# Which engine makes the low parts of split weights: GpSimd and VectorE together, or VectorE alone

## The chip, the cores and the metric

The kernel runs on one core of a Trainium2 chip. The metric is device time in microseconds (us), the median of three runs; the profile comes from one further execution, whose own time is given beside it. Five engines work at once, each with its own queue of instructions, which it takes in order: TensorE (PE in the rows; PEld is its loading of weights), VectorE (DVE), ScalarE (ACT), GpSimd (POOL) and SyncE (SP), which here only starts transfers from memory.

## The reference, cut to what matters

256 rows of width 1024 go through two blocks of two layers each, all in float32.

```python
def first_block(x, mem, ...):
    for l in range(2):
        h = rms_norm(x, mix_norm_g[l])
        u, v, q, k, vv = split(h @ w_in[l])
        gm = gmlp_group(gelu(u), gelu(v), ...)
        at = gqa_group(q, k, vv, q_norm_g, k_norm_g, cos, sin)   # normed, rotated, softmax
        x = x + concat(rms_norm(gm), rms_norm(at)) @ w_out[l]
        x = x + memory_cross_attention(rms_norm(x), mem_n, ...)
        x = x + expert_choice_moe(rms_norm(x), ...)              # 16 experts
def second_block(x, c, ...):
    for l in range(2):
        sh1, sc1, g1, ... = split(silu(c) @ w_mod[l] + b_mod[l])
        x = x + 0.5 * g1 * swiglu(rmsnorm(x) * (1 + sc1) + sh1, ffn1 weights)
        x = x + g2 * hybrid_mixer(rmsnorm(x) * (1 + sc2) + sh2, ...)
        x = x + 0.5 * g3 * swiglu(rmsnorm(x) * (1 + sc3) + sh3, ffn2 weights)
```

The hybrid mixer multiplies the normed rows by w_in and feeds three groups of heads: stick-breaking attention, dilated attention (q and k normed by head and rotated, then three softmax patterns in one) and a gated recurrence (HGRN2), whose decays are worked out in seven levels of halving distance.

## The kernel before, in words

**Split products.** A dense product of two float32 matrices is made of three matrix products in a faster format: `mm3` (L134 to L140) adds high by high (L138), the one operand's low part by the other's high part (L139), and high by low (L140). A weight comes from memory in pieces of 1 MB (128 partitions of 2048 numbers) into a slot of a ring (`load`, L82). `split_w` (L108 to L132) cuts a piece into four parts of 128x512: ScalarE copies each into the high part (`wh`, L126), and VectorE or GpSimd subtracts that from the slot to give the low part (`wl`, L129). The high and low tiles come from a pool of 7 pairs in the first block and 8 in the second: a new pair waits until TensorE has done the products of the pair 7 or 8 places before it. The experts' weights are used unsplit, so they have no low parts.

**Who makes the low parts.** `lo_engines` (L94 to L103) gives the four engines of a piece. A pattern in `lo_on["first"]` is used once; else `lo_on["pool"]` pieces go to GpSimd whole; else the next letter of `lo_on["w"]` counts, V for VectorE, P for GpSimd, M for taking turns. `norm_T`, the norm ahead of a dense product, sets `lo_on["pool"]` to 1 (NP), so the first piece behind it goes to GpSimd.

**What else is on these engines.** VectorE also runs the chains of small operations ahead of attention: `root` (an inverse square root by three rounds of L185 to L189 on tiles of 128x1, 128x16 or 128x20), the diagonal matrices of a norm (L312, `diag`, which TensorE multiplies by the rows at L322), the put-away of a norm's result (L263, L265), the rotation (L567 to L589 in the first block, L1155 to L1169 in the hybrid mixer), the softmax's scaling (L501, L1207, `xn`) and the recurrence's products (L1289, L1290) and masked copies into the score matrix (L1273, L1300, `ST`). GpSimd also makes the recurrence's differences (L1286, L1287), the last sums of the row of modulations (L431), small powers (L176) and starts small transfers.

**Order.** A scheduler puts each engine's instructions into an order when the kernel is built, by its own estimates of durations; the code only names some that must come behind others (`queued`). An engine never passes a waiting instruction.

Of the kernel before, what the change touches and what calls it, by code (L numbers as in the profile page):

```python
# [34 lines left out]
L1, L2, NP = 1, 2, 1  # L35
# [6 lines left out]
def kernel(ctx: ExitStack, tc: tile.TileContext, A: dict, out: bass.AP, phases=None):  # L42
    nc = tc.nc
    V, ACT, PE, POOL = nc.vector, nc.scalar, nc.tensor, nc.gpsimd
# [9 lines left out]
    def dense_scope(stack, name):  # L54

        scope["split"] = stack.enter_context(tc.tile_pool(name=f"split{name}", bufs=8, reuse_waits="tile"))
        h = stack.enter_context(tc.tile_pool(name=f"h{name}", bufs=1, reuse_waits="tile"))
        scope["h"], scope["turn"] = [h, h], 0
# [29 lines left out]
    lo_on = {"w": "VP", "n": 0, "t": 0}  # L88
# [179 lines left out]
    def hl(name):  # L268
        pools, i = scope["h"], scope["turn"]
        scope["turn"] = 1 - i  # L270
        return tuple(
            pools[i].tile([P, KC, S], F32R, tag="hT" + e, name=uid(name + e), bufs=1 + (pools[0] is pools[1]))
            for e in "hl"
        )
# [24 lines left out]
    def norm_T(src, g, sh=None, gap=0, site="b", by_row=True, pre=None, row=None):  # L299


        h = hl("hT")
        lo_on["pool"] = NP
        dg = []
        sqs = h[1].rearrange("p (t n k) s -> p t n (k s)", t=2, n=2)
        if row is None:
# [210 lines left out]
    def mix(l, kT, v):  # L517
        with tc.tile_pool(name=f"mix{l}", bufs=1, reuse_waits="tile") as wk:
            w = A["w_in"][l]
            lo_on["first"] = 'PPVV'  # L520
            h, pre = raw_T(
                x, vec[:, 8 * l : 8 * l + 8], GM * l, l == 0, lambda: weights(w, 0, KC, 1536, 256)
            )
# [33 lines left out]
            if l == 0:  # L557
                mh, _ = norm_T(mem_load(), vec[:, 32:40], site="e")
# [468 lines left out]
    def late_init(pool):  # L1027

        t = pool.tile([P, NLATE], F32, name="late")
        POOL.dma_start(out=t, in_=A["const"][:, NKEEP:])  # L1030
        masks = pool.tile([P, NMASK], U8, name="masks").rearrange("p (n t) -> p n t", n=8)
        m = slot()[:, :NMASK]
        POOL.dma_start(out=m, in_=A["masks"])
        V.tensor_copy(masks, m.rearrange("p (n t) -> p n t", n=8))
        take = taker(t)
        return [take(P), take(P), masks] + [take(n, t=2) for n in (2 * S, 2 * S, 64, 64)]
# [24 lines left out]
    def ffn(l, name, q):  # L1061
        ms, mc = mod[l]
        wg, wu, wd = (A[f"{name}_w_{e}_2"][l] for e in ("gate", "up", "down"))
        with tc.tile_pool(name=f"{name}{l}", bufs=2, reuse_waits="tile") as wk:
            scale, row, gap = mc[:, 8 * q + 8 : 8 * q + 16], None, GB
            if l == q == 0:
                scale = small.tile([P, KC], F32, tag="gsc", name="gsc", bufs=1)
                V.tensor_tensor(scale, vec[:, 88:96], mc[:, 8:16], ALU.mult)
                row, gap = final_row[0], GF
            h, pre = norm_T(x, scale, mc[:, 8 * q : 8 * q + 8], gap, "b", q != 6, lambda: columns(wg, 0), row)  # L1070
            g = wk.tile([P, D], F32, tag="gate", name=uid("gate"), bufs=1)
            acc = [ps("acc") for _ in range(4)]
# [45 lines left out]
    def hybrid(l, tables):  # L1118
        ms, mc = mod[l]
        tri, sbneg, masks, dil_c, dil_neg, d_cos, d_sin = tables  # L1120
        w = A["w_in_2"][l]
        with tc.tile_pool(name=f"hyb{l}", bufs=1, reuse_waits="tile") as wk:
            h, pre = norm_T(
                x, mc[:, 32:40], mc[:, 24:32], max(GB, due(32 + 36 * l)), "h",
                pre=lambda: weights(w, 0, 4, 768, 512),
# [309 lines left out]
    side = {KV0: kv_begin} | {KV0 + 1 + i: kv_step(i) for i in range(8)}  # L1435

    for l in range(2):
        lo_on["w"] = 'VPVPVPVPVPVPVPVPVPVPVPVPVPV'
        lo_on["n"] = 0
        with ExitStack() as more:  # L1440
            with ExitStack() as st:
                split = st.enter_context(tc.tile_pool(name=f"split{l}", bufs=7, reuse_waits="tile"))
# [33 lines left out]
    with ExitStack() as st:  # L1476
        late = st.enter_context(tc.tile_pool(name="late", bufs=1, reuse_waits="tile"))
        dense_scope(st, "b")
        for l in range(2):
            lo_on["w"] = "V"  # L1480
            ffn(l, "ffn1", 0)
            if l == 0:
                tables = late_init(late)
            lo_on["w"] = 'VVVPVPVPVVVVVVVMVV'
            lo_on["n"] = 0
            hybrid(l, tables)
            lo_on["w"] = "V"
            ffn(l, "ffn2", 6)
# [119 lines left out]
```

## Time and profile before

| | |
|---|---|
| three runs, median (lowest to highest) | 2527.57 us (2526.87 to 2528.56) |
| the profiled execution: its own time, its span | 2528.26 us, 2526.2 us |
| busy: TensorE, VectorE, ScalarE, GpSimd | 86%, 49%, 39%, 19% |
| mean granted clock of TensorE | 0.918 |

By place, in us from the span's start: the first layer's mixer and cross attention take 0 to 240, its experts 240 to 735; the second layer's mixer and cross attention 735 to 912, its experts to 1385. In the second block the parts ffn1, hybrid mixer, ffn2 end at 1575, 1755 and 1950 in the first layer, and at 2153, 2332 and 2526 in the second. A row of the timeline gives start, duration, engine, line, operation, tiles and count, and in brackets how long the engine had been idle and what ended that. A row of waits gives engine, line, what was waited for, the sum in us, how many times, and the longest. Matmul ends are modelled, so a chain of matmuls is read from their starts.

### The profile page before, as it was taken

The numbers are of one execution on the slowest core, as the hardware profiler recorded it, in microseconds if no ns is written. First come the engines' busy times: TensorE is split into PE (matmuls) and PEld (weight loads), VectorE is DVE, ScalarE is ACT, GpSimd is POOL, SyncE is SP. The second block draws the span as 40 slices with busy tenths as digits, with TensorE's granted clock in tenths as the row PEclk, the third lists the DMA queues.
The fourth block names the chain that finished last, engine by engine and source line by source line (L and its number), as shares of the span: only waits on it lengthen the run. The fifth ranks groups of instructions, "written<-read, shape, count | busy, mean of one in ns | idle before, by whom it ended". The sixth has DMA issues, their size and how long they took to land.

```text
span 2526.2 us, 39105 instructions
## 1 busy us (share of the span) xinstructions
PE 2164.4 (86%) x15752; PEld 1614.4 (64%) x15752; DVE 1236.4 (49%) x2295; ACT 975.2 (39%) x1830; POOL 484.4 (19%) x328
## 2 busy tenths in 40 slices
PE   7898867787686987766667999999999999889999
PEld 6787424443165853212213998877998999777998
DVE  6755101000055531000003986877895986877655
ACT  5553110000044521000003774555764864545654
POOL 5141000000031300000001641231641550241100
PEclk9999979888888999878778999899999999989999
DMA  7367999999971789999997885424885785523652
GB/s 282 104 264 317 396 419 420 420 419 420 420 310 65 287 353 419 420 420 420 420 420 311 318 299 197 167 78 153 305 298 180 297 293 193 187 95 137 232 185 84
DMA packets 100214, 721.37 MB, mean 286 GB/s; under 512 B 11471, under 2 KB 11599, under 8 KB 12993
## 3 DMA queue, kind: packets, MB, share of 16 engines
q1 hardware_dynamic: 98640, 715.70, 72.5%
q0 software_dynamic: 1104, 3.06, 0.5%
q8 instruction: 124, 2.03, 0.3%
q14 instruction: 58, 0.47, 0.1%
q10 hardware_dynamic: 288, 0.12, 0.0%
HBM read 717.78 MB, written 1.05 MB: 285 GB/s over the span
## 4 chain that ended last, share of the span: by engine, by line
PE 53%; DMA 32%; DVE 10%; ACT 2%; issue 2%; POOL 0%; SPq 0%; ACTq 0%; DVEq 0%; POOLq 0%
DMA slot<-in_w_up_dram 11%; PE w L139 11%; PE w L138 11%; PE w L140 11%; DMA slot<-in_w_down_dram 9%; DMA slot<-in_w_gate_dram 8%; PE acc L138 3%; PE acc L139 3%; PE acc L140 3%; DMA slot<-in_xattn_w_kv_dram 2%; DVE wl L129 2%; PE w L926 2%; PE w L961 1%; PE acc L1297 1%; PE w L322 1%
## 5 line engine op out<-in xcount | busy, mean ns | idle before, releaser
L129 DVE TENSOR_TENSOR wl<-slot,wh 128x512 fp32r<-128x512 f32 x712 | 618.6, 901 | 219.8 <-ACT wh L126 206.4
L126 ACT ACTIVATE wh<-slot 128x512 fp32r<-128x512 f32 x856 | 514.5, 628 | 283.5 <-PE w L140 148.6
L139 PE MATMUL w<-hTh,wl 128*128 128x256 f32 x1792 | 512.2, 286 | 1.6 <-DVE wl L129 1.6
L140 PE MATMUL w<-hTl,wh 128*128 128x256 f32 x1792 | 511.3, 285 | 2.2 <-DVE hTl L265 2.2
L138 PE MATMUL w<-hTh,wh 128*128 128x256 f32 x1792 | 511.4, 285 | 1.8 <-ACT wh L126 1.8
L926 PE MATMUL w<-slot,XgT 128*32 128x256 f32 x4096 | 308.5, 434 | 140.9 <-DMA slot<-in_w_up_dram 103.7
L129 POOL TENSOR_TENSOR wl<-slot,wh 128x512 fp32r<-128x512 f32 x144 | 196.1, 1384 | 805.6 <-ACT wh L126 728.7
L138 PEld LDWEIGHTS w<-hTh,wh 128*128 128x128 f32 x1792 | 345.3, 193 | 7.9 <-issue 2.7
L139 PEld LDWEIGHTS w<-hTh,wl 128*128 128x128 f32 x1792 | 345.5, 193 | 7.0 <-DVE wl L129 4.0
L140 PEld LDWEIGHTS w<-hTl,wh 128*128 128x128 f32 x1792 | 345.4, 193 | 4.6 <-DVE hTl L265 3.7
L926 PEld LDWEIGHTS w<-slot,XgT 128*32 128x32 f32 x4096 | 123.9, 120 | 319.5 <-DMA slot<-in_w_up_dram 163.2
L950 DVE TENSOR_TENSOR a<-a,w 128x256 f32<-128x256 f32 x32 | 13.5, 421 | 521.2 <-ACT a L950 521.2
L961 PE MATMUL w<-slot,aT 128*32 128x512 f32 x1024 | 162.0, 724 | 44.5 <-DMA slot<-in_w_down_dram 26.3
L950 ACT ACTIVATE a<-w 128x256 f32<-128x256 f32 x32 | 12.3, 384 | 476.7 <-PE w L926 467.6
L431 POOL TENSOR_TENSOR mprod<-mprod 128x1024 f32<-128x1024 f32 x44 | 112.9, 2567 | 171.8 <-ACT mprod L430 171.8
L138 PE MATMUL acc<-wh,ah 128*128 128x512 f32 x352 | 138.5, 393 | 0.0
L139 PE MATMUL acc<-wh,al 128*128 128x512 f32 x352 | 137.3, 390 | 0.0
L140 PE MATMUL acc<-wl,ah 128*128 128x512 f32 x352 | 137.1, 389 | 0.0
L430 ACT ACTIVATE mprod<-slot,cm 128x512 f32<-128x512 f32 x176 | 119.5, 714 | 40.1 <-DMA slot<-in_w_mod_dram 38.0
L961 PEld LDWEIGHTS w<-slot,aT 128*32 128x32 f32 x1024 | 30.9, 121 | 152.6 <-DMA slot<-in_w_down_dram 82.9
L138 PE MATMUL w<-wh,hTh 128*128 128x512 f32 (+1 forms) x320 | 119.9, 375 | 5.8 <-DVE hTl L260 5.8
L140 PE MATMUL w<-wl,hTh 128*128 128x512 f32 (+1 forms) x320 | 119.0, 373 | 6.4 <-DVE wl L129 6.4
(392 smaller groups left out, 2913.0 us busy)
## 6 DMA issues: line engine op xcount, KB each, us to landing
slot<-in_w_gate_dram SPq DMA_DIRECT2D x128, 1024.0 KB, 19.9
slot<-in_w_up_dram SPq DMA_DIRECT2D x128, 1024.0 KB, 19.9
slot<-in_w_down_dram SPq DMA_DIRECT2D x128, 1024.0 KB, 19.9
slot<-in_w_mod_dram SPq DMA_DIRECT2D x72, 1024.0 KB, 5.5
slot<-in_ffn_w_gate_dram SPq DMA_DIRECT2D x44, 1024.0 KB, 5.3
slot<-in_ffn_w_up_dram SPq DMA_DIRECT2D x44, 1024.0 KB, 5.1
slot<-in_ffn_w_down_dram SPq DMA_DIRECT2D x44, 1024.0 KB, 5.1
slot<-in_w_in_dram SPq DMA_DIRECT2D x42, 1024.0 KB, 6.8
```

Source lines behind the costliest of these rows:

```text
L126: lead["act"] = ACT.activation(hi, r[:, c], AF.Copy)
L129: low = eng[i].tensor_tensor(lo, r[:, c], hi.bitcast(F32), ALU.subtract)
L138: PE.matmul(o, a[0], b[0], start=start, stop=False, skip_group_check=True)
L139: PE.matmul(o, a[1], b[0], start=False, stop=False, skip_group_check=True)
L140: lead["pe"] = PE.matmul(o, a[0], b[1], start=False, stop=stop, skip_group_check=True)
L322: PE.matmul(pt[:, i, t * P : (t + 1) * P], src[:, t, c * P : (c + 1) * P], dg[t], start=t == 0 and i == 0, stop=True, skip_group_check=True,)
L430: ACT.activation(f[:, i], raw[:, i], AF.Copy, scale=cm[:, ka + i, 31:32])
L431: POOL.tensor_tensor(f[:, :2], f[:, :2], f[:, 2:], ALU.add)
L926: PE.matmul(gu[CAP * g : CAP * g + CAP, 256 * wi : 256 * wi + 256], XgT[:, e // 4 % 2, k, e % 4 * CAP : e % 4 * CAP + CAP], raw[:, kk, 256 ...
L950: past = [ACT.activation(a, gu[:, :256], AF.Silu), V.tensor_tensor(a, a, gu[:, 256:], ALU.mult)]
L961: PE.matmul(py[CAP * g : CAP * g + CAP], aT[:, j, CAP * i : CAP * i + CAP], raw, start=i == 0, stop=i == 3, skip_group_check=True, tile_po ...
L1297: PE.matmul(pt[:, i], segs(E)[:, i], upper(segs(E)[:, i]), start=True, stop=True, skip_group_check=True)
```

## The change

All low parts outside the first piece now go to VectorE: `norm_T` sends no piece to GpSimd any more, the first block's mixers and the hybrid mixers get the letter V alone, and the one-time pattern of the first piece (two parts on GpSimd, two on VectorE) is kept for layer 0 only. Of GpSimd's 144 low parts 142 move: 52 in the first block's layer 0, 38 in layer 1, 4 in each of the four feed-forward networks and 18 in each of the two hybrid mixers. Lines behind L520 count one more, so L1175 before is L1176 after.

```diff
--- before.py
+++ after.py
@@ -300,7 +300,7 @@
 
 
         h = hl("hT")
-        lo_on["pool"] = NP
+        lo_on["pool"] = 0
         dg = []
         sqs = h[1].rearrange("p (t n k) s -> p t n (k s)", t=2, n=2)
         if row is None:
@@ -517,7 +517,8 @@
     def mix(l, kT, v):
         with tc.tile_pool(name=f"mix{l}", bufs=1, reuse_waits="tile") as wk:
             w = A["w_in"][l]
-            lo_on["first"] = 'PPVV'
+            if l == 0:
+                lo_on["first"] = 'PPVV'
             h, pre = raw_T(
                 x, vec[:, 8 * l : 8 * l + 8], GM * l, l == 0, lambda: weights(w, 0, KC, 1536, 256)
             )
@@ -1435,8 +1436,7 @@
     side = {KV0: kv_begin} | {KV0 + 1 + i: kv_step(i) for i in range(8)}
 
     for l in range(2):
-        lo_on["w"] = 'VPVPVPVPVPVPVPVPVPVPVPVPVPV'
-        lo_on["n"] = 0
+        lo_on["w"] = "V"
         with ExitStack() as more:
             with ExitStack() as st:
                 split = st.enter_context(tc.tile_pool(name=f"split{l}", bufs=7, reuse_waits="tile"))
@@ -1481,8 +1481,6 @@
             ffn(l, "ffn1", 0)
             if l == 0:
                 tables = late_init(late)
-            lo_on["w"] = 'VVVPVPVPVVVVVVVMVV'
-            lo_on["n"] = 0
             hybrid(l, tables)
             lo_on["w"] = "V"
             ffn(l, "ffn2", 6)
```

The scheduler orders everything anew. Three places show it.

VectorE, layer 0, the rotation of q and k (`qk`, normed by `rq` and multiplied by the gains `G`); the low part `wl_467` is one that TensorE is waiting for. Before:

```order
L567 TENSOR_TENSOR qk_168<-qk_168,rq_615 128x1280
L129 TENSOR_TENSOR wl_467<-slot_452,wh_466 128x512
L569 TENSOR_TENSOR qk_168<-qk_168,G_354 128x512
L570 TENSOR_TENSOR qk_168<-qk_168,G_354 128x128
L569 TENSOR_TENSOR qk_168<-qk_168,G_354 128x512
L570 TENSOR_TENSOR qk_168<-qk_168,G_354 128x128
L577 TENSOR_TENSOR sq_613<-qk_168,cst 128x320
```

After:

```order
L568 TENSOR_TENSOR qk_168<-qk_168,rq_615 128x1280
L129 TENSOR_TENSOR wl_467<-slot_452,wh_466 128x512
L129 TENSOR_TENSOR wl_497<-slot_494,wh_496 128x512
L129 TENSOR_TENSOR wl_501<-slot_494,wh_500 128x512
L129 TENSOR_TENSOR wl_505<-slot_494,wh_504 128x512
L129 TENSOR_TENSOR wl_509<-slot_494,wh_508 128x512
L570 TENSOR_TENSOR qk_168<-qk_168,G_354 128x512
L571 TENSOR_TENSOR qk_168<-qk_168,G_354 128x128
L570 TENSOR_TENSOR qk_168<-qk_168,G_354 128x512
L571 TENSOR_TENSOR qk_168<-qk_168,G_354 128x128
```

The four parts of the next piece (slot_494), which GpSimd made before, now stand between the scaling and the gains.

VectorE, first hybrid mixer, the inverse square roots `rq` of the dilated attention's heads. Before:

```order
L1153 TENSOR_REDUCE rq_11473<-h_2006_11471 128x16
L129 TENSOR_TENSOR wl_11625<-slot_11610,wh_11624 128x512
L194 TENSOR_SCALAR ms_11475<-rq_11473 128x16
L180 TENSOR_SCALAR nw_11477<-ms_11475 128x16
L181 TENSOR_SCALAR nw_11477<-ms_11475 128x16
L182 TENSOR_SCALAR nw_11477<-nw_11477 128x16
L187 TENSOR_TENSOR nw_11477<-nw_11477 128x16
L188 TENSOR_TENSOR nw_11477<-nw_11477 128x16
L189 SCALAR_TENSOR_TENSOR nw_11477<-nw_11477 128x16
L187 TENSOR_TENSOR nw_11477<-nw_11477 128x16
L188 TENSOR_TENSOR nw_11477<-nw_11477 128x16
L189 SCALAR_TENSOR_TENSOR nw_11477<-nw_11477 128x16
```

After:

```order
L194 TENSOR_SCALAR ms_11475<-rq_11473 128x16
L129 TENSOR_TENSOR wl_11625<-slot_11610,wh_11624 128x512
L180 TENSOR_SCALAR nw_11477<-ms_11475 128x16
L181 TENSOR_SCALAR nw_11477<-ms_11475 128x16
L129 TENSOR_TENSOR wl_11682<-slot_11679,wh_11681 128x512
L182 TENSOR_SCALAR nw_11477<-nw_11477 128x16
L129 TENSOR_TENSOR wl_11686<-slot_11679,wh_11685 128x512
L187 TENSOR_TENSOR nw_11477<-nw_11477 128x16
L129 TENSOR_TENSOR wl_11690<-slot_11679,wh_11689 128x512
L188 TENSOR_TENSOR nw_11477<-nw_11477 128x16
L129 TENSOR_TENSOR wl_11694<-slot_11679,wh_11693 128x512
L189 SCALAR_TENSOR_TENSOR nw_11477<-nw_11477 128x16
```

GpSimd made the four parts of slot_11679 beside this chain before; now they stand between its steps.

TensorE, the same mixer, at the first transposes of the rotated q and k (`m_2010`), which wait for the chain above. Before:

```order
L139 MATMUL w_11609<-hTh_11191,wl_11625 128x256
L140 MATMUL w_11609<-hTl_11192,wh_11624 128x256
L138 MATMUL w_11609<-hTh_11191,wh_11624 128x256
L1175 MATMUL acc_11507<-cst,m_2010_11491 128x128
L1175 MATMUL acc_11513<-cst,m_2010_11491 128x128
L139 MATMUL w_11609<-hTh_11191,wl_11625 128x256
```

After:

```order
L139 MATMUL w_11678<-hTh_11191,wl_11686 128x256
L140 MATMUL w_11678<-hTl_11192,wh_11685 128x256
L138 MATMUL w_11678<-hTh_11191,wh_11685 128x256
L1176 MATMUL acc_11507<-cst,m_2010_11491 128x128
L1176 MATMUL acc_11513<-cst,m_2010_11491 128x128
L139 MATMUL w_11678<-hTh_11191,wl_11686 128x256
```

Before, the transposes stood behind 43 of the 48 matrix products of w_11609; now behind all 48 and 22 of w_11678.

VectorE, the same mixer, the recurrence: products of level 1 to 3 (`h_2111`, `h_2113`, `h_2115`), then copies into the score matrix `ST`. Before:

```order
L1289 TENSOR_TENSOR h_2111_12126<-h_2111_12126,kh_11606 128x8x64
L1290 TENSOR_TENSOR h_2111_12126<-h_2111_12126,qh_11607 128x8x64
L1289 TENSOR_TENSOR h_2113_12142<-h_2113_12142,kh_11606 128x16x32
L1290 TENSOR_TENSOR h_2113_12142<-h_2113_12142,qh_11607 128x16x32
L1289 TENSOR_TENSOR h_2115_12158<-h_2115_12158,kh_11606 128x32x16
L1290 TENSOR_TENSOR h_2115_12158<-h_2115_12158,qh_11607 128x32x16
L129 TENSOR_TENSOR wl_12314<-slot_12299,wh_12313 128x512
L129 TENSOR_TENSOR wl_12344<-slot_12341,wh_12343 128x512
L1273 COPY_PREDICATED ST_12112<-masks,acc_12114 128x512
L129 TENSOR_TENSOR wl_12348<-slot_12341,wh_12347 128x512
L1273 COPY_PREDICATED ST_12112<-masks,acc_12120 128x512
L129 TENSOR_TENSOR wl_12352<-slot_12341,wh_12351 128x512
```

After:

```order
L129 TENSOR_TENSOR wl_12344<-slot_12341,wh_12343 128x512
L129 TENSOR_TENSOR wl_12348<-slot_12341,wh_12347 128x512
L1290 TENSOR_TENSOR h_2111_12126<-h_2111_12126,kh_11606 128x8x64
L1291 TENSOR_TENSOR h_2111_12126<-h_2111_12126,qh_11607 128x8x64
L1274 COPY_PREDICATED ST_12112<-masks,acc_12114 128x512
L1274 COPY_PREDICATED ST_12112<-masks,acc_12120 128x512
L1290 TENSOR_TENSOR h_2113_12142<-h_2113_12142,kh_11606 128x16x32
L1301 COPY_PREDICATED ST_12112<-masks,acc_12132 128x8x64
L1291 TENSOR_TENSOR h_2113_12142<-h_2113_12142,qh_11607 128x16x32
```

The first two copies moved from behind three levels and two low parts to behind the first level. On TensorE, the products of the levels now stand among those of the next piece, one level at a time, where before the first three stood in a row; and between the last transposed values of the dilated attention (L1220, L1221 after) and the recurrence's first scores there are 85 matrix products where there were 110.

## Rows read from the trace of the kernel before

**Rows 1.** Groups of the page: L129; out<-in xcount | busy, mean ns | idle, releaser.

```profile
L129 DVE TENSOR_TENSOR wl<-slot,wh 128x512 fp32r<-128x512 f32 x712 | 618.6, 901 | 219.8 <-ACT wh L126 206.4
...
L129 POOL TENSOR_TENSOR wl<-slot,wh 128x512 fp32r<-128x512 f32 x144 | 196.1, 1384 | 805.6 <-ACT wh L126 728.7
```

**Rows 2.** Instructions on tile wl: ns min/median/max, first and last start.

```profile
L129 DVE TENSOR_TENSOR wl<-slot,wh x712: 641/692/2929, 10.7 to 2511.0; 128x512 fp32r<-128x512 f32 x178
```

**Rows 3.** Timeline of VectorE, layer 0, rotation of q and k.

```profile
44.56 0.18 DVE L188 TENSOR_TENSOR nw<-nw 128x20 f32<-128x20 f32 x1
...
46.24 1.22 DVE L188 TENSOR_TENSOR nw<-nw 128x20 f32<-128x20 f32 x1
...
...
51.14 1.75 DVE L129 TENSOR_TENSOR wl<-slot,wh 128x512 fp32r<-128x512 f32 x1
```

**Rows 4.** Waits of TensorE, 45 to 60 us.

```profile
PE w L140 <- DVE wl L129: 4.9, 1, 4.9
```

**Rows 5.** Timeline of VectorE, the first block's two softmax scalings in layer 0.

```profile
76.65 6.24 DVE L501 TENSOR_SCALAR xn<-xn,den 128x256 f32<-128x256 f32 x8
...
96.64 2.19 DVE L501 TENSOR_SCALAR xn<-xn,den 128x256 f32<-128x256 f32 x8
```

**Rows 6.** Waits of TensorE, 70 to 125 us.

```profile
PE acc L650 <- issue: 4.1, 1, 4.1
PE acc L511 <- ACT wh L126: 2.4, 1, 2.4
PE acc L511 <- DVE xn L501: 2.2, 3, 0.9
```

**Rows 7.** Timeline of VectorE ahead of L650: one of four such rows.

```profile
106.76 1.22 DVE L189 SCALAR_TENSOR_TENSOR nw<-nw 128x1 f32<-128x1 f32 x1
```

**Rows 8.** Waits of TensorE, layer 1, 735 to 815 us.

```profile
PE w L140 <- DVE wl L129: 1.6, 1, 1.6
```

**Rows 9.** Waits of TensorE in the first hybrid mixer, 1575 to 1755 us.

```profile
PE w L322 <- DVE diag L312: 6.1, 3, 3.1
PE acc L1297 <- DVE ST L1273: 4.8, 1, 4.8
PE acc L1175 <- DVE m L1169: 4.2, 1, 4.2
...
PE acc L1212 <- DVE xn L1207: 1.7, 3, 0.8
PE acc L1297 <- DVE h L1290: 0.8, 1, 0.8
```

**Rows 10.** Timeline of VectorE at that mixer's norm, its two diagonals.

```profile
1575.49 1.36 DVE L312 TENSOR_SCALAR diag<-cst,rms 128x128 f32<-128x128 f32 x1
...
1578.94 0.29 DVE L312 TENSOR_SCALAR diag<-cst,rms 128x128 f32<-128x128 f32 x1
```

**Rows 11.** Timeline of TensorE around L1175: products at the lower and the higher clock.

```profile
1612.09 0.41 PE L139 MATMUL w<-hTh,wl 128*128 128x256 f32 x1
1612.30 0.41 PE L140 MATMUL w<-hTl,wh 128*128 128x256 f32 x1
...
1616.10 0.28 PE L138 MATMUL w<-hTh,wh 128*128 128x256 f32 x1
1616.22 0.28 PE L139 MATMUL w<-hTh,wl 128*128 128x256 f32 x1
```

**Rows 12.** Timeline of ScalarE: the exponential from which the recurrence's chain starts.

```profile
1649.30 1.06 ACT L1242 ACTIVATE h<-h 128x1024 f32<-128x1024 f32 x1
```

**Rows 13.** Timeline of VectorE in the recurrence.

```profile
1658.50 1.56 DVE L1290 TENSOR_TENSOR h<-h,qh 128x512 f32<-128x512 f32 x1
...
1665.94 3.20 DVE L129 TENSOR_TENSOR wl<-slot,wh 128x512 fp32r<-128x512 f32 x2
```

**Rows 14.** Stretches: us, busy PE, PEld, DVE, ACT, POOL, clock, DMA share, GB/s.

```profile
240.00:740.00 500.00, 377.38 (x3289) 193.86 (x3280) 64.42 (x191) 49.01 (x110) 13.71 (x15) 0.87 1.00 412
740.00:762.00 22.00, 20.45 (x90) 16.61 (x90) 20.40 (x45) 12.76 (x20) 9.21 (x8) 1.00 0.49 177
```

## The prediction

> **What bounds the kernel now.** I read the page's groups first, then the waits of TensorE stretch by stretch, then VectorE's timeline just ahead of each wait. A low part takes 692 ns of VectorE at the median, yet 901 on the mean of its 712, and 1384 of GpSimd on the mean of 144 [rows 1, 2]. The timeline says where the difference comes from: with GpSimd's subtractions running beside it, an operation of 128x20 that takes 0.18 us takes 1.22, and a low part 1.75 [rows 3]. TensorE is the engine that the time follows. In the experts (240 to 740 us and again in layer 1) it waits for memory, whose share is 1.00 [rows 14], and no low part matters there. Elsewhere it is full but for waits of 1 to 6 us, nearly all on such VectorE chains [rows 4, 6, 8, 9]. So the question is what these waits become, not how much VectorE or GpSimd work in all.
>
> **The change, part by part.** 142 low parts at 0.69 us are 98 us more for VectorE. Against that it loses most of the time in which it is held up; GpSimd keeps only the modulation sums and the recurrence's differences, which go on colliding. A negative sign is time saved.
>
> *Layer 0, rotation.* TensorE waits 4.9 us for one low part [rows 4]. In the chain before that part four operations read 1.16 to 1.22 where 0.18 is their time, and the part itself 1.75 in place of 0.69: 4 x 1.02 + 1.06 = 5.1 us [rows 3]. That covers the wait. Four low parts (2.8 us) enter this chain, but by the order behind the part that is waited for; the rotation's own end then moves by 5.1 - 2.8, still forward. -4.9. After such a wait the products run at the lower of the two clock levels (1.2 GHz) for some us: in the hybrid mixer their starts are 0.21 us apart then, and 0.12 later [rows 11]; over 16 products that is 1.4 us, an estimate that I take for this wait as well. -1.4.
>
> *Layer 0, softmax.* Eight scalings take 6.24 us beside GpSimd's parts and 2.19 without [rows 5]. TensorE's waits there sum to 4.6 [rows 6]; the three between the scalings (2.2) go, and of the first one the 1.0 us by which the first scaling is longer. -3.2.
>
> *Layer 0, ahead of L650.* Four operations of 128x1 or 128x2 take 1.2 us in place of 0.2 [rows 7], 4.1 us on the chain, and TensorE's wait at L650 is 4.1 [rows 6]. By the new order more products also stand ahead of it. -4.1. Layer 0 in sum: -13.6. Bounds: -4.9 if only the first goes, -18 with the clock of the other two places. What hides it could be the experts' stream: that is a rival, below.
>
> *Layer 1.* One wait of 1.6 us on a low part [rows 8]. In this chain VectorE is busy 20.40 of 22 us [rows 14], so removed collisions (about 5 us, five of them at 1.0 as in [rows 3]) stand against eight more parts, 5.5 us, of which half lie in idle time. -1.5, bounds -4 to +3.
>
> *Feed-forward norms, four of them.* The second diagonal is held up as the first in [rows 10] (1.07 us). The four parts (2.8 us) come onto VectorE between the diagonal and the put-away, where it has been waiting for TensorE and where the put-away's own collisions go. I take -0.5 each, -2.0; bounds -4 to +6 (1.5 us each if the parts are not covered).
>
> *Hybrid norms, two.* Four operations of some 1.2 to 1.36 us precede the second diagonal [rows 10], about 4.2 us too long; four parts (2.8) take their place. -1.5 each, -3.0; bounds -5 to +3.
>
> *Dilated attention, first transposes.* TensorE waits 4.2 us [rows 9]. Here the low parts on VectorE eat what the collisions gave: four operations at 1.2 us go, six parts come, and each also needs ScalarE's high part, so the chain ends only some 0.6 us earlier, an estimate from lining the new order up with the parts' times. But 27 more matrix products (48 + 22 against 43) stand ahead, 27 x 0.12 = 3.2 us [rows 11]. 4.2 - 0.6 - 3.2 leaves 0.4. -3.7 for each mixer, and -1.4 for the clock behind it, read there [rows 11]. -10.2; bounds -12 to 0.
>
> *Dilated softmax.* 1.7 us of waits on the scaling L1207 [rows 9], held up like L501. -1.5 each, -3.0.
>
> *Recurrence.* Now 4.8 us of waiting at the third level, since the first copy into the score matrix stands behind three levels and two low parts that take 3.20 us [rows 13, 9], and 0.8 more at the second level. The new order puts that copy behind the first level: that wait goes. But a new one comes. From the start of ScalarE's exponential at 1649.30 to the end of the first level's product at 1658.50 + 1.56 it is 10.8 us [rows 12, 13]. By the new order that exponential stands behind high parts which need their tiles back from TensorE's 36th product of a piece, so it starts some 5.2 us behind the last transposed values, an estimate: 25 products at 0.12 [rows 11], then a high part and the loading of a function table, some 2 us; the level is ready at 5.2 + 10.8 = 16.0. TensorE gets there after 85 products (10.2 us) and the first scores (1.8): 12.0. The wait is 4.0 where 5.6 was. -1.6 each, -3.2; bounds -11 (all of both waits) to +6.
>
> **The sum.** 13.6 + 1.5 + 2.0 + 3.0 + 10.2 + 3.0 + 3.2 = 36.5 us. On the profiled execution's own 2528.26 that is 2491.8; the median of the runs lies 0.7 lower, 2527.57 - 36.5 = 2491.
>
> **The rivals.** *The in-order queue takes back what the collisions gave.* The low parts now stand among the steps of the chains, and a part that waits for its tile or its high part holds everything behind it. The row of two parts in the recurrence that held a copy for 3.20 us [rows 13] shows this; the new order puts six among the `rq` steps. Then the hybrid mixers and feed-forward networks bring nothing, and layers 0 and 1 remain: 2527.57 - 15.1 = 2512. Against it: TensorE has products to do while these parts wait, by the new order more than before. The Trainium skill ("TensorE: Matmul & The Clock Gate", architectural detail, engine queue depths) calls VectorE's queue strictly first in, first out; the trace agrees, in that no row of it passes another.
>
> *VectorE becomes the bound (slower).* The place is the mixers of both blocks, where 60 of the moved parts (36 in the hybrids, 16 in the feed-forward norms, 8 in layer 1's chain) stand in latency chains. Each of these that lies on the path costs 0.69. From 27 of the 60 on it eats layer 0's 13.6 and 5 us more. At 45 of 60: 45 x 0.69 = 31, less 13.6, gives +17.5: 2545. For it: 20.40 of 22 us busy in layer 1's chain [rows 14]. Against it: outside such stretches VectorE is idle half the time, and the collisions that go were on the same chains. The Trainium skill ("Perfetto Trace Analysis", Optimizing Scalar/DVE Operations) speaks for this rival: handing work to GpSimd may make sense where VectorE is saturated, though the shared port may undo it. The rows show both sides: saturation in a few stretches, and a price of 1.0 us for a collision, more than the 0.69 that a handed-over part saves.
>
> *The experts' stream hides it.* If the transfers of the experts started at a time of their own, layer 0 and 1 would gain nothing: 2506 alone, and with the first rival no change, 2527. Against it: slots come free by TensorE's work, and memory moves at 412 GB/s [rows 14] only from the experts on.
>
> That the change does not do what it says is excluded by the order.
>
> **How the numbers follow.** The forecast, 2491 with its own range of 2475 to 2508 (the terms' bounds taken half together, and the stream alone): 0.60. The queue, 2512: 0.17. No change, 2527: 0.09. VectorE the bound, 2545: 0.14. What a measurement of this kernel can tell from no change is about 0.2%, 5 us. Faster 0.60 + 0.17 = 0.77, same 0.09, slower 0.14. The range for 8 in 10 takes in the forecast, the queue's 2512 and what lies up to the edge of no change: 2474 to 2522.
>
> **What would show it.** In the profile after: GpSimd's group on L129 gone to 2, VectorE's mean on L129 near 0.7 but in the stretches of the modulation sums; L187 to L189 at 0.18 everywhere outside the recurrence. Right: the waits of [rows 4] and on L650 and L1175 gone, L1212's as well, and in the recurrence a wait of some 4 us at the first level's scores. Wrong in the first rival's way: the wait at L1176 stays near 4 us, and VectorE's idle time ahead of a low part grows, put down to ScalarE's `wh`. Wrong in the second's: TensorE waits for low parts (L139, L140 on `wl`) and for diagonals longer than 6.1 in a mixer. The forecast fails as a whole if the times of layer 0 shrink and the experts still end at the same time.

## The result and the profile after

The changed kernel takes 2469.19 us (median; 2468.53 to 2470.55), the kernel before, run beside it, 2528.07 (2526.87 to 2531.71): a ratio of 0.9766, 95% interval 0.9754 to 0.9778. That is 58.9 us saved where 36.5 were forecast, so the direction held and the time lies 5 us below the range. The profiled execution took 2468.85 us with a span of 2466.8; the mean granted clock of TensorE is 0.925 (0.918 before).

The page of the changed kernel, busy time and the group of L129 (columns as in [rows 1]):

```profile
PE 2148.9 (87%) x15752; PEld 1595.8 (65%) x15752; DVE 1249.9 (51%) x2437; ACT 974.1 (39%) x1828; POOL 290.4 (12%) x186
...
L129 DVE TENSOR_TENSOR wl<-slot,wh 128x512 fp32r<-128x512 f32 x854 | 695.1, 845 | 196.0 <-ACT wh L126 190.9
```

VectorE took over 142 low parts, which at 0.69 us are 98 us of work, and is busy only 13.5 us longer (1236.4 before): the rest it had spent held up. GpSimd's busy time fell by 194 us (484.4 before). TensorE has the same 15752 products and is busy 15.5 us less (2164.4 before).

The stretches of two places, first layer's mixer and first hybrid mixer (start and end, us, then busy us and count of PE, PEld, DVE, ACT, POOL, the granted clock, DMA share, GB/s). The kernel before:

```profile
0.00:248.80 248.80, 218.45 (x1287) 185.75 (x1287) 151.12 (x407) 127.85 (x283) 82.85 (x70) 0.94 0.63 242
1573.80:1749.20 175.40, 156.38 (x960) 135.84 (x960) 136.16 (x253) 94.89 (x158) 44.29 (x35) 0.91 0.38 132
```

The changed kernel:

```profile
0.00:230.20 230.20, 211.67 (x1287) 180.59 (x1288) 160.50 (x459) 128.23 (x283) 9.09 (x18) 0.98 0.68 261
1548.10:1707.60 159.50, 149.10 (x961) 127.83 (x960) 129.16 (x271) 93.87 (x158) 19.92 (x16) 0.98 0.42 145
```

In such a row the stretch less PE's busy time is what TensorE waits. In the mixer of layer 0 it waits 30.35 us before and 18.53 after, and its products, the same in number, take 218.45 and then 211.67. In the hybrid mixer 19.02 and 10.40, and 156.38 and 149.10. Both parts of the gain stand in these two stretches; the whole program cut at the same instructions gives:

| place | span before, after | change | of it waits | of it products | forecast |
|---|---|---|---|---|---|
| layer 0: mixer, cross attention | 248.8, 230.2 | -18.6 | -11.8 | -6.8 | -13.6 |
| its experts | 469.2, 469.2 | 0.0 | -5.4 | +5.4 | 0 |
| layer 1: mixer, cross attention | 197.9, 195.7 | -2.2 | -2.1 | -0.1 | -1.5 |
| its experts | 454.7, 451.0 | -3.7 | -3.9 | +0.2 | 0 |
| four feed-forward parts | 805.9, 801.5 | -4.4 | -4.1 | -0.3 | -2.0 |
| first hybrid mixer | 175.4, 159.5 | -15.9 | -8.6 | -7.3 | -9.7 |
| second hybrid mixer | 174.3, 159.7 | -14.6 | -8.0 | -6.6 | -9.7 |
| sum | 2526.2, 2466.8 | -59.4 | -43.9 | -15.5 | -36.5 |

The waits of TensorE in the changed kernel (engine, line, what for, sum us, times, longest), in layer 0 at the places of [rows 4] and [rows 6]:

```profile
PE acc L511 <- ACT wh L126: 1.3, 1, 1.3
PE acc L612 <- ACT qkT L600: 0.7, 1, 0.7
PE acc L612 <- ACT xn L496: 0.2, 1, 0.2
```

and in the first hybrid mixer, where [rows 9] had 6.1, 4.8, 4.2 and 1.7 us (1.8 of the 6.1 belong to the norm behind the mixer; the mixer's own two diagonals had 4.3):

```profile
PE acc L1298 <- DVE h L1291: 5.5, 3, 4.7
PE w L322 <- DVE diag L312: 1.2, 2, 0.7
PE acc L1349 <- ACT m L1342: 1.0, 1, 1.0
PE w L138 <- ACT wh L126: 0.9, 1, 0.9
PE acc L1405 <- DVE o L1402: 0.7, 2, 0.4
PE acc L1213 <- DVE xn L1208: 0.4, 1, 0.4
```

The wait for the low part in layer 0's rotation is gone, those on the softmax's scaling and ahead of L650 too; 1.3 us for a high part stay. In the mixer the waits for the first transposes and for the masked copy are gone, and a new one of 4.7 us stands at the recurrence's first level. One more wait shrank that [rows 9] leaves out; L1405 had 2.6 us before, as L1404:

```profile
PE acc L1404 <- DVE o L1401: 2.6, 2, 2.1
```

VectorE in the changed kernel (start, us, line, operation; count at the end): the rotation, softmax and first mixer's norm and `rq` chain, to be read beside [rows 3], [rows 5] and [rows 10].

```profile
42.06 0.18 DVE L188 TENSOR_TENSOR nw<-nw 128x20 f32<-128x20 f32 x1
...
44.54 3.09 DVE L129 TENSOR_TENSOR wl<-slot,wh 128x512 fp32r<-128x512 f32 x5
...
70.28 2.19 DVE L501 TENSOR_SCALAR xn<-xn,den 128x256 f32<-128x256 f32 x8
...
1570.62 0.17 DVE L187 TENSOR_TENSOR nw<-nw 128x16 f32<-128x16 f32 x1
1570.70 0.68 DVE L129 TENSOR_TENSOR wl<-slot,wh 128x512 fp32r<-128x512 f32 x1
1571.31 0.17 DVE L188 TENSOR_TENSOR nw<-nw 128x16 f32<-128x16 f32 x1
```

No operation of these chains is held up any more, the five low parts in the rotation run through in 3.09 us, and those between the steps of `rq` cost 0.68 each.

### The profile page after: what moved, and what is told of

It reads as the page before. It is cut to its first block, busy times and chain, and to the rows that moved or that the text cites. A ratio compares the mean times of both kernels' runs of the same rounds, so it can differ in the third digit from the quotient of the medians.

```text
span 2466.8 us, 39054 instructions
## 1 busy us (share of the span) xinstructions
PE 2148.9 (87%) x15752; PEld 1595.8 (65%) x15752; DVE 1249.9 (51%) x2437; ACT 974.1 (39%) x1828; POOL 290.4 (12%) x186
## 3 DMA queue, kind: packets, MB, share of 16 engines
HBM read 717.78 MB, written 1.05 MB: 291 GB/s over the span
## 4 chain that ended last, share of the span: by engine, by line
PE 56%; DMA 32%; DVE 6%; ACT 3%; issue 2%; POOL 0%; SPq 0%; DVEq 0%; ACTq 0%; POOLq 0%
PE w L139 12%; PE w L140 12%; PE w L138 12%; DMA slot<-in_w_up_dram 11%; DMA slot<-in_w_down_dram 11%; DMA slot<-in_w_gate_dram 8%; PE acc L138 3%; PE acc L139 3%; PE acc L140 3%; DMA slot<-in_xattn_w_kv_dram 2%; PE w L927 2%; DVE wl L129 1%; PE acc L1298 1%; DMA slot<-in_w_in_dram 1%; PE w L962 1%
## 5 line engine op out<-in xcount | busy, mean ns | idle before, releaser
L129 DVE TENSOR_TENSOR wl<-slot,wh 128x512 fp32r<-128x512 f32 x854 | 695.1, 845 | 196.0 <-ACT wh L126 190.9
L138 PE MATMUL w<-hTh,wh 128*128 128x256 f32 x1792 | 508.8, 284 | 3.1 <-DVE putf L263 2.0
L140 PE MATMUL w<-hTl,wh 128*128 128x256 f32 x1792 | 509.8, 285 | 0.0
L927 PE MATMUL w<-slot,XgT 128*32 128x256 f32 x4096 | 320.0, 447 | 127.4 <-DMA slot<-in_w_up_dram 93.8
L138 PEld LDWEIGHTS w<-hTh,wh 128*128 128x128 f32 x1792 | 343.4, 192 | 8.4 <-ACT hTh L264 2.5
L140 PEld LDWEIGHTS w<-hTl,wh 128*128 128x128 f32 x1792 | 343.4, 192 | 2.8 <-issue 1.5
L951 DVE TENSOR_TENSOR a<-a,w 128x256 f32<-128x256 f32 x32 | 13.5, 421 | 521.8 <-ACT a L951 521.8
L962 PE MATMUL w<-slot,aT 128*32 128x512 f32 x1024 | 153.9, 693 | 51.5 <-DMA slot<-in_w_down_dram 33.2
L138 PE MATMUL acc<-wh,ah 128*128 128x512 f32 x352 | 138.5, 393 | 0.0
L140 PE MATMUL acc<-wl,ah 128*128 128x512 f32 x352 | 137.1, 389 | 0.0
L138 PE MATMUL w<-wh,hTh 128*128 128x512 f32 (+1 forms) x320 | 118.1, 370 | 8.3 <-DVE hTl L260 6.5
L140 PE MATMUL w<-wl,hTh 128*128 128x512 f32 (+1 forms) x320 | 117.6, 369 | 0.0
L139 PE MATMUL w<-wh,hTl 128*128 128x512 f32 (+1 forms) x320 | 117.5, 367 | 0.0
```

What stands on the lines that cost most here:

```text
L129: low = eng[i].tensor_tensor(lo, r[:, c], hi.bitcast(F32), ALU.subtract)
L138: PE.matmul(o, a[0], b[0], start=start, stop=False, skip_group_check=True)
L139: PE.matmul(o, a[1], b[0], start=False, stop=False, skip_group_check=True)
L140: lead["pe"] = PE.matmul(o, a[0], b[1], start=False, stop=stop, skip_group_check=True)
L927: PE.matmul(gu[CAP * g : CAP * g + CAP, 256 * wi : 256 * wi + 256], XgT[:, e // 4 % 2, k, e % 4 * CAP : e % 4 * CAP + CAP], raw[:, kk, 256 ...
L951: past = [ACT.activation(a, gu[:, :256], AF.Silu), V.tensor_tensor(a, a, gu[:, 256:], ALU.mult)]
```

## The experiments

**Theories.** The first: the gain is the collisions of GpSimd's subtractions with VectorE's chains; what waits they took is returned, and then some, by TensorE's clock. The rival: the collisions matter little, and the gain is the new order, which puts more products in front of the waits. A third question is the new wait at the recurrence: how much is left there.

### The change in three parts

The first block's part alone (p_first) leaves `norm_T` and the hybrid mixers as before:

```diff
-            lo_on["first"] = 'PPVV'
+            if l == 0:
+                lo_on["first"] = 'PPVV'
...
-        lo_on["w"] = 'VPVPVPVPVPVPVPVPVPVPVPVPVPV'
-        lo_on["n"] = 0
+        lo_on["w"] = "V"
```

> Only the first block's part of the change: the mixers' letter V and the one-time pattern for layer 0 alone; norms and hybrid mixers as before. Theory (each part's gain is local and carries through): layer 0 gave 18.3 us, layer 1 and the experts behind it 5.7 in the changed kernel's trace, so 24 us less than before, about 2504. Rival (the experts' stream hides the first block's gain, and the 59 us come from elsewhere): within 5 us of before, 2528.

Measured: 2504.26 beside 2528.66 for the kernel before (0.990, 0.9876 to 0.9924): -24.4, as expected. The gain is less local than the theory has it, though: in the trace the first block ends 19.7 us earlier, and the second block, which this edit does not name, is shorter too (1151.2 us where the kernel before has 1155.6).

The norms' part alone (p_norm):

```diff
-        lo_on["pool"] = NP
+        lo_on["pool"] = 0
```

> Only the norms' part: no whole piece to GpSimd behind a norm; all patterns of letters as before. Theory (collisions at the norm's chain): the hybrid norms gave 5.4 us each in the changed kernel's trace and the feed-forward norms some 4 in all, so 15 us less, about 2513. Rival (in-order queue: the four parts on VectorE lengthen the norm's chain, and the gain needs the rest of the change): no change or up to 10 us slower.

Measured: 2498.46 (0.9876, 0.9861 to 0.9891): -30.2, twice what was expected. The edit is not a pure part: in the mixers the pattern's letters now count from the first piece, so GpSimd's parts sit on other pieces and the order changes with them. In its first hybrid mixer TensorE waits:

```profile
PE acc L1175 <- DVE m L1169: 5.9, 1, 5.9
PE w L322 <- DVE diag L312: 1.9, 3, 0.8
PE acc L1297 <- DVE h L1290: 1.7, 1, 1.7
```

The wait for the masked copy, 4.8 us in [rows 9], has left with the order, not with a collision: the copies stand right behind the three levels there, without the two low parts of [rows 13], while most products of the levels still take 1.5 us.

The hybrid mixers' letters alone (p_hyb):

```diff
-            lo_on["w"] = 'VVVPVPVPVVVVVVVMVV'
-            lo_on["n"] = 0
```

> Only the hybrid mixers' letter V; norms and first block as before. Theory: behind the norm the two mixers gave 11.5 and 10.5 us in the changed kernel's trace, so 22 us less, about 2506. Rival (the parts only help together, since one leaves GpSimd's other parts to collide): under 10 us less.

Measured: 2507.49 (0.9913, 0.9897 to 0.993): -21.2, as expected. The three parts together would be 75.8 us where the whole change gives 59. They overlap in the second block, which takes 1155.6 us before, 1151.2, 1126.7 and 1136.1 in the traces of the three, and 1120.7 with the whole change: each edit has everything ordered anew, and p_norm and p_hyb both change what runs beside the mixers' chains. So the split by edits names no cause, and the next kernels hold the order fixed.

### The same order, with the collisions put back

In x_read every instruction of TensorE, VectorE and ScalarE stands in the order of the changed kernel. In the second block alone GpSimd repeats the 52 subtractions that it made before, into a spare tile that nobody reads; this work is added to what the reference asks for.

```diff
-                low = eng[i].tensor_tensor(lo, r[:, c], hi.bitcast(F32), ALU.subtract)
+                spare = scope.get("spare") if eng[i] is POOL else None
+                low = (V if spare is not None else eng[i]).tensor_tensor(lo, r[:, c], hi.bitcast(F32), ALU.subtract)
+                if spare is not None:
+                    POOL.tensor_tensor(spare, r[:, c], hi.bitcast(F32), ALU.subtract)
```

> The changed kernel, with all of VectorE's, ScalarE's and TensorE's instructions in the same order; only in the second block GpSimd repeats, into a spare tile that nobody reads, the 52 subtractions that it made before (feed-forward norms 16, hybrid mixers 36). Theory (collisions lengthened the chains, and waits and clock followed): most of the second block's 35 us comes back, 15 to 35 us more than the changed kernel's 2469. Rival (the new order made the gain: more products stand ahead of the waits): within 5 us of 2469.

Measured: 2522.53 (2518.16 to 2526.23; 0.9978, 0.9968 to 0.9988 of the kernel before), 53 us more than the changed kernel, where 15 to 35 were expected. In the trace the second block grows from 1120.7 to 1171.1, 50.4 us: 12.5 on products and 37.9 on waits. VectorE, with the same instructions, is busy 48.4 us longer there (871.74, then 920.17). The first block, where nothing is repeated, ends 5.2 us later in this execution; that part does not belong to the subtractions. The waits of its first hybrid mixer:

```profile
PE acc L1179 <- DVE m L1173: 5.5, 1, 5.5
PE acc L1301 <- DVE h L1294: 5.5, 3, 4.7
PE w L325 <- DVE diag L315: 4.5, 2, 3.8
PE acc L1408 <- DVE o L1405: 2.8, 2, 1.5
PE acc L1216 <- DVE xn L1211: 2.2, 2, 1.5
```

The timelines of VectorE in that mixer's `rq` chain and of GpSimd beside it:

```profile
1586.45 1.29 DVE L190 TENSOR_TENSOR nw<-nw 128x16 f32<-128x16 f32 x1
1587.67 0.68 DVE L130 TENSOR_TENSOR wl<-slot,wh 128x512 fp32r<-128x512 f32 x1
1588.27 1.29 DVE L191 TENSOR_TENSOR nw<-nw 128x16 f32<-128x16 f32 x1
```

```profile
1583.93 7.41 POOL L132 TENSOR_TENSOR spare<-slot,wh 128x512 bf16<-128x512 f32 x4 [21.13 <-ACT wh L126]
```

The operation of 0.17 us is at 1.29 again. The first transposes (L1179) wait 5.5 us although the same products as in the changed kernel stand in front of them: in the chain ahead of them four operations take 1.28 to 1.30 in place of 0.17 and a low part 1.75 in place of 0.69, 5.5 us in all. The diagonals are back at 4.5. So the collisions carry the gain in this block: with them put back, the new order alone brings nothing, 1171.1 us against the 1155.6 that the kernel before has from the same place on. The 15.5 us between these two hold what the 52 more parts on VectorE cost and also the collisions that these parts meet themselves, so 50.4 is the price of the collisions in the new order; their price in the old one was not measured apart. ScalarE's longest waits in x_read, 7.2 and 7.1 us for a high part, are no cause of their own: the first ends at 1600.51, behind the products that follow the first transposes (1599.30) on TensorE, and GpSimd's last read before that had ended at 1595.48.

x_write has the same orders and the same 52 places, but GpSimd reads one column there and then only writes:

```diff
+                    POOL.tensor_tensor(spare[:, :1], r[:, c][:, :1], hi.bitcast(F32)[:, :1], ALU.subtract)
+                    for _ in range(2):
+                        POOL.memset(spare, 0.0)
```

> As x_read, with VectorE, ScalarE and TensorE in the same order as in the changed kernel, but in place of each of the 52 spare subtractions GpSimd reads one column (128x1) and then fills the spare tile twice with zeros: as many starts of about the same busy time in sum, which write and hardly read. Theory (it is GpSimd's reading of SBUF that holds VectorE): within 12 us of the changed kernel's 2469, for the small reads. Rival (any busy GpSimd does it, by its writes or by the waits that it adds): most of x_read's 53 us, over 2500.

Measured: 2469.94 (2468.97 to 2472.11; 0.9777, 0.9756 to 0.9798): the changed kernel's time. GpSimd is busy 360.30 us in the second block, more than x_read's 356.24, yet VectorE is busy 873.36 us there against the changed kernel's 871.74 and TensorE's products take 1088.86 against 1088.77, in 1121.3 us against 1120.7. The `rq` chain with two memsets running beside it, VectorE and then GpSimd:

```profile
1575.46 0.17 DVE L193 TENSOR_TENSOR nw<-nw 128x16 f32<-128x16 f32 x1
1575.66 0.17 DVE L194 SCALAR_TENSOR_TENSOR rq<-nw 128x16 f32<-128x16 f32 x1
```

```profile
1575.54 1.11 POOL L134 MEMSET spare<- 128x512 bf16 x2
```

It is the reading that holds VectorE up, not GpSimd's being busy. The Trainium skill ("SBUF — State Buffer", Who interferes with whom) says that a VectorE instruction with both inputs in SBUF contends with a GpSimd instruction that reads SBUF and not with one that only writes. The trace agrees: 1.29 us beside the first, 0.17 beside the second.

x_half is x_read with each subtraction in two halves of 128x256, to see whether a shorter hold is a cheaper one:

```diff
+                    for k in (0, 256):
+                        POOL.tensor_tensor(spare[:, k : k + 256], r[:, c][:, k : k + 256], hi.bitcast(F32)[:, k : k + 256], ALU.subtract)
```

> x_read with each spare subtraction of 128x512 cut into two of 128x256; all other engines in the same order again. If a VectorE operation is held only until the GpSimd instruction that runs ends, holds are half as long but can be twice as many: where operations follow each other closely the cost stays, 2515 to 2525; if each chain meets only so many holds, half of x_read's 53 us goes, 2490 to 2500.

Measured: 2513.48 (2510.07 to 2517.07; 0.9943, 0.993 to 0.9957); 44 of the 53 us remain, a little less than the first expectation and far from the second. The `rq` chain:

```profile
1578.82 0.73 DVE L191 TENSOR_TENSOR nw<-nw 128x16 f32<-128x16 f32 x1
...
1582.11 0.66 DVE L191 TENSOR_TENSOR nw<-nw 128x16 f32<-128x16 f32 x1
```

A hold is half as long (0.73), but more operations meet one: VectorE is busy 41.4 us longer in the second block than in the changed kernel, where x_read's was 48.4, and L1180 still waits 5.4 us. Nor is it the length of GpSimd's instruction that sets x_write apart: a half subtraction takes 0.72 us at its shortest, a memset 0.53.

### The wait that is left: the recurrence

TensorE in the changed kernel at the first two levels, and GpSimd's differences before them:

```profile
1625.39 3.64 PE L1298 MATMUL acc<-h 128*128 128x64 f32 x16 [4.66 <-DVE h L1291]
...
1631.90 1.89 PE L1298 MATMUL acc<-h 128*128 128x64 f32 x16
```

```profile
1617.69 2.51 POOL L1287 TENSOR_TENSOR h<-G 128x512 f32<-128x512 f32 x1 [71.51 <-DVE G L1248]
1620.17 1.05 POOL L1288 TENSOR_TENSOR h<-G 128x512 f32<-128x512 f32 x1
```

After the wait of 4.66 us the same 16 products take 3.64 us, and 1.89 at the next level. And here GpSimd is the one that is held: 2.51 us for what is 1.05 alone.

Three kernels move these differences to VectorE: those of level 1 (r_one), all seven levels (r_all), and every second level (r_alt, levels 1, 3, 5, 7). The edit, for r_alt:

```diff
-                LV = {"P": (POOL, POOL), "V": (V, V), "M": (POOL, V)}['PPPPPPP'[n]]
+                LV = {"P": (POOL, POOL), "V": (V, V), "M": (POOL, V)}['VPVPVPV'[n]]
```

> The changed kernel with the recurrence's first level of differences (two of 14 operations) made by VectorE too. Theory: the first level's chain at the wait of 4.66 us has two GpSimd operations of 2.51 and 1.05 us in a row, which VectorE would do in 1.4, so the wait falls by 2 us, and the clock behind it gives some 1 us back: 2 mixers x 3 = 6 us less, 2463. Rival (the wait is set by TensorE's and ScalarE's order, not by GpSimd): no change, 2469.

Measured: 2468.77 (2463.22 to 2469.40; 0.9767, 0.9747 to 0.9786). In the trace, which is of the fastest of its four executions (2463.22), the wait at level 1 falls from 4.66 to 2.18, and two others come, 1.71 at a later level and 1.5 for a high part (0.9 in the changed kernel): no change that can be measured.

> The changed kernel with all 14 differences of a recurrence made by VectorE, so that GpSimd reads SBUF in the mixers no more but for two small parts. If collisions are all that counts: the products L1290 and L1291 take 0.69 us throughout and the wait of 4.66 shrinks, 8 to 12 us less, 2457 to 2461. Rival (VectorE becomes the bound of a level: four operations at 0.69 and a copy at 0.72, 3.5 us, against 3.0 between levels now): 6 levels x 0.5 x 2 mixers = 6 us more behind the first level, so no better than 2466.

Measured: 2466.4 (2465.01 to 2471.68; 0.9766, 0.9746 to 0.9786), as the rival has it. In the trace, of the slowest of its four executions, the first wait falls to 0.69 and another of 3.95 comes at a later level: no change either.

> The changed kernel with levels 1, 3, 5 and 7 of the recurrence's differences on VectorE and the others left on GpSimd. If GpSimd's three us between two levels set the pace there, sharing them takes 1 us off every second level, 3 levels x 1 x 2 mixers: 6 us less than the changed kernel. If TensorE's products between the levels set it: within 3 us.

Measured: 2457.85 (2457.00 to 2463.70; 0.973, 0.9717 to 0.9743). The changed kernel, run again on the same chip (a_same), beside it:

> The changed kernel itself, beside which the other three of this call are read on the same chip: 2466 to 2472.

Measured: 2468.81 (2467.92 to 2474.29; 0.9771, 0.9758 to 0.9784). So r_alt is 11 us faster, where 6 were expected, and beats both kernels. Its waits in the first hybrid mixer:

```profile
PE acc L1298 <- DVE h L1291: 1.6, 2, 1.3
PE acc L1336 <- issue: 1.4, 1, 1.4
PE acc L1349 <- ACT m L1342: 1.2, 1, 1.2
```

The stretch around the recurrence (columns as above), in the changed kernel and then in r_alt:

```profile
1620.00:1640.00 20.00, 14.79 (x90) 13.48 (x89) 14.03 (x16) 8.05 (x11) 14.87 (x13) 0.83 0.11 46
```

```profile
1620.00:1640.00 20.00, 18.65 (x132) 16.77 (x130) 17.88 (x26) 11.13 (x15) 9.27 (x6) 1.00 0.16 53
```

TensorE gets 132 products done in these 20 us against 90, with the clock at full. From the first recurrence's scores to the second's the two kernels differ by 7.5 us, from there to the end by 4.3. What did it is not settled: r_alt's order also puts eight products and L474 between the scores and level 1. r_one's order has them there too, with a wait of 2.18 us and no gain; but no run holds r_alt's order with the differences on GpSimd.

x_fill tries the clock by itself: six products (12 instructions in the trace, 5.32 us) into a tile that is written over afterwards, work that the reference does not ask for, stand in front of level 1, so that TensorE does not idle there.

```diff
+                if n == 0:
+                    with queued([lead["pe"]]):
+                        for _ in range(6):
+                            PE.matmul(pt, ident, x[:, 0, :512], start=True, stop=True, skip_group_check=True)
```

> The changed kernel with six idle matrix products (128x512, into a tile that the level's own products then overwrite) put ahead of the recurrence's first level, where TensorE now waits 4.66 us; nothing is computed otherwise. Theory (a wait costs more than itself, since the products behind it run at the lower of the two clock levels for some us): the wait is filled, TensorE stays at the higher level, and the products behind gain 2 to 3 us per mixer: 2463 to 2466 although TensorE does 8 us more. Rival (the lower clock is not the wait's doing, or costs nothing): 2469 or more.

Measured: 2481.4 (2478.82 to 2484.29; 0.9822, 0.9803 to 0.9841), 12 us more than the changed kernel; the expectation missed. TensorE at later levels, and two stretches:

```profile
1628.32 1.89 PE L1303 MATMUL acc<-h 128*128 128x64 f32 x16
...
1639.77 2.71 PE L1303 MATMUL acc<-h 128*128 128x64 f32 x16 [3.26 <-DVE h L1291]
```

```profile
1620.00:1640.00 20.00, 16.45 (x102) 12.74 (x102) 16.76 (x20) 10.00 (x12) 16.65 (x12) 1.00 0.31 106
1640.00:1652.00 12.00, 12.00 (x55) 11.42 (x55) 5.97 (x9) 1.78 (x3) 2.49 (x2) 0.53 0.00 0
```

The filler did what it was put there for: level 1's 16 products take 1.89 us in place of 3.64, and the clock holds. But the scheduler also put two levels in a row, so a wait of 3.26 us came at 1636.5, and behind it 12 us at 0.53, near the lower of the two levels (1.2 of 2.4 GHz). The price of the clock alone is therefore not measured by this kernel. The wait of 4.66 us in the changed kernel and this one of 3.26 were each followed by a stretch at the lower level. A shorter one need not be: r_one's wait of 2.18 us has a granted clock of 1.00 in the 6.8 us behind it in the first mixer and of 0.64 in the second.

## Why the prediction was right in direction and short in size

**The bound and the waits: right.** Outside the experts TensorE's waits fell by 34.7 us; the forecast, without its clock terms, was 32.3. Place by place: layer 0 11.8 against 12.2; layer 1 2.1 against 1.5; feed-forward parts 4.1 against 2.0; the two hybrid mixers together 16.6 against 16.6. That this last pair agrees is luck, as the next lines show. The transposes' wait was put at 0.4 and is gone. The masked copy's wait went and a new one of 4.66 us came at the recurrence's first level, forecast as 4.0. The norms were better than thought (TensorE waits 1.2 us for a mixer's diagonals, 3.1 less, forecast 1.5 less), the recurrence worse (5.5 in all, forecast 4.0), 1.9 us at L1405 went that the forecast does not list, and two waits on ScalarE came (1.0 and 0.9).

**The clock: the term that failed.** The prediction gave "-1.4" to three places, 4.2 us in all, an estimate from 16 products after one wait. The products outside the experts took 21.0 us less: 6.8 in layer 0, 7.3 and 6.6 in the hybrid mixers, 0.3 elsewhere. The three places are layer 0's rotation and the two mixers' first transposes. At the softmax, ahead of L650, at the hybrid norms and at the masked copy the prediction put the clock at nothing, and the kernel before stood at the lower level there as well. Its stretches at the rotation, the softmax, L650, the norm's diagonals and the masked copy (columns as in [rows 14]; the granted clock is 1.00 at the higher level and 0.50 at the lower, so a mean between them has both in it):

```profile
52.00:56.00 4.00, 3.06 (x7) 2.46 (x8) 4.00 (x9) 0.64 (x1) 1.00 (x2) 0.57 0.48 147
79.00:87.00 8.00, 6.22 (x36) 5.34 (x37) 5.40 (x11) 1.49 (x4) 2.68 (x3) 0.57 0.63 230
117.00:121.00 4.00, 4.00 (x15) 3.46 (x14) 1.94 (x5) 0.00 (x0) 0.00 (x0) 0.57 0.07 27
1578.00:1586.00 8.00, 6.78 (x31) 6.44 (x31) 6.48 (x20) 2.86 (x7) 0.50 (x1) 0.57 1.00 356
1667.00:1677.00 10.00, 7.08 (x27) 6.53 (x28) 10.00 (x14) 1.82 (x3) 4.21 (x3) 0.50 0.60 209
```

In the changed kernel the granted clock is 1.00 from 30 to 147.7 us and from 1547 to 1618.8, up to the wait at the recurrence. It agrees in size in the mixer: a mean of 0.91 over 175.4 us is 31.6 us at the lower level, 0.98 over 159.5 is 6.4; of the 25.2 us less, 8.6 are waits, and the products in the other 16.6 run in half the time, 8.3 us less where 7.3 were measured. For layer 0 the same sum gives 4.4 against 6.8; the clock's rounding to 0.01 alone moves it by 2. So the lower level went with nearly every wait of a chain, not with those of three places, and lasted longer than 16 products: in the changed kernel's recurrence it shows on L138 to L140 too, whose products of 128x512 start 0.43 us apart until 1631.4, six us behind the wait, and 0.23 apart in x_fill, where the clock held. In the experts, where memory sets the pace (share 1.00 and 1.01), products even took 5.5 us more and the waits gave it back: a loss on products does not show in the time there.

With 21.0 in place of 4.2 the sum is 53.3 of the traces' 59.4, and the time 2474. Of the other 6.1 us, 2.4 are the waits above and 3.7 the second experts' stretch. The prediction put the experts at nothing. That stretch takes 454.7 us in the three kernels with the first block's old letters (before, p_norm, p_hyb) and 450.1 to 451.0 in the ten with the new ones, so it belongs to the change; what shortened it no run shows.

**The range.** Its low end, 2474, is said to come from the terms' bounds half together. Worked again, the better bounds of all terms add to 57.0 us: half of what they add to the forecast gives 2481, all of it 2471. So the low end does not follow from the bounds, and even all of them at once do not reach 2469: no bound but layer 0's held a clock beyond the three places. That is the same step.

**The rivals.** The in-order queue: six parts do stand among the `rq` steps and none waits; from L1153 to the end of the multiplication by `rq` the chain takes 8.5 us where it took 9.7. VectorE the bound: in the second block its 52 new parts are 36 us of work at 0.69, and TensorE's waits and products there still fell by 34.9 us in sum; what the parts cost by themselves no run measures apart from the collisions (the 15.5 us of x_read hold both). The Trainium skill ("Perfetto Trace Analysis", Optimizing Scalar/DVE Operations) grants that handing work to GpSimd may help a saturated VectorE and warns that the shared port may undo it; here the warning holds, by 2.3% of the time. The experts' stream hides it: layer 0's end moved by 18.6 us and the first experts took 469.2 both times, so they started that much earlier.

**What is argued and not shown.** That layer 0's gain is collisions, as in the second block, rests on its rows (1.22 to 0.18 us) and on the 19.7 us by which p_first ends that block earlier; no run put the collisions back there.

## What to carry to other kernels

An engine that looks half idle is not free help: 52 subtractions of GpSimd, whose results nobody reads, cost 50 us in the block where they stand, by holding up chains of 0.17 us operations, so first look in the timeline for short operations with long durations beside another engine's. Price a wait of TensorE with what follows it: outside the experts each us of wait removed brought 0.6 us more from the clock (21.0 to 34.7), but only 0.3 where the order stayed the same (x_read, 12.5 to 37.9). To tell contention from reordering, keep the order and add the suspected work into a tile that nobody reads; splitting the change by its edits did not tell them apart.

## What the runs showed of the hardware

Either engine can be the one that is held: one of GpSimd's differences took 4.32 us in r_alt, in place of 1.05, while VectorE ran a row of operations with two inputs.

```profile
1618.66 4.32 POOL L1287 TENSOR_TENSOR h<-G 128x512 f32<-128x512 f32 x1 [71.50 <-DVE G L1248]
1622.95 1.08 POOL L1288 TENSOR_TENSOR h<-G 128x512 f32<-128x512 f32 x1
```

In x_write a GpSimd read of a single column took between 0.19 and 2.36 us in the first hybrid mixer, the longest while VectorE ran its products of the rotation. Halving the reads halved each hold (1.29 to 0.73 us) and left five sixths of the cost. Operations with one input were held as well: the diagonal of 128x128 took 1.36 us beside subtractions [rows 10] and 0.29 alone. Memsets are not quite without effect on these: in x_write a scaling of 128x128 (L1213) took 0.63 us in place of 0.28 beside two memsets, once in each mixer.
